# All 18 input projection blocks of a layer in 512-column products by twos, and six weight subtractions on GpSimd

## The chip, the cores and the metric

The kernel runs on one core of a Trainium2 chip. The metric is the device time of one execution, in microseconds (us). A core has a matrix engine (TensorE, in the profile PE, with its weight loads as PEld), three engines for elementwise work (VectorE or DVE, ScalarE or ACT, GpSimd or POOL), and SyncE (SP), which here issues the transfers. Each engine takes its instructions in its own order and waits at semaphores for the others. SBUF is the on-chip memory; PSUM holds the banks that TensorE writes into.

## What is computed

Two decoder layers over 256 tokens of width 1024. Each layer multiplies x by one wide input matrix and cuts the product into ten parts for three groups of heads: retention (rq, rk, rv, rg), softmax attention with a bias (mq, mk, mv) and a short convolution (cb, cc, ch). The group results go through an output matrix and a LayerNorm, then through a gated MLP and a second LayerNorm. Cut to what matters here:

```python
def hybrid_mixer(h, w_in, conv_w, w_out, rel_bias):
    proj = h @ w_in
    rq, rk, rv, rg, mq, mk, mv, cb, cc, ch = parts      # columns of proj
    q_r = rotary(split_heads(rq)); k_r = rotary(split_heads(rk)) * scale
    y_ret = merge_heads(head_group_norm(retention(q_r, k_r, v_r))) * silu(rg)
    y_moba = merge_heads(moba_attention(split_heads(mq), split_heads(mk), split_heads(mv), rel_bias))
    y_conv = cb * causal_dwconv(cc * ch, conv_w)
    return concatenate([y_ret, y_moba, y_conv]) @ w_out

def reference(x, ...):
    for l in range(2):
        x = layer_norm(ALPHA * x + hybrid_mixer(x, ...), ln1_g[l], ln1_b[l])
        x = layer_norm(ALPHA * x + conv_ffn(x, ...), ln2_g[l], ln2_b[l])
    return x
```

## The kernel before

The products keep fp32 accuracy by taking each operand as two parts in a shorter format: hi, a cast on ScalarE (`split`, line 81), and lo, what is left, a subtraction on VectorE (line 82). A product is then hi·hi + hi·lo + lo·hi. The tokens x lie in one tile `xx` of 128 rows x 8 k x 2 parts x 256 tokens; `xh` and `xl` are its two parts.

The weights come as a list of units of up to 128x1024. `prepare` (line 120) loads and converts units in the order of that list: a transfer on SP into one of five `raw` buffers, then `convert` (line 115) with `split` into one of six `whi` and six `wlo` buffers. `weights` (line 143) hands out one unit and prepares up to five units ahead.

Of each layer's input products, 18 are blocks of 128 features by 256 tokens (`FBLK`: mq0 to mq2, mk0 to mk2, then rq and rk by turns, then ch0, cc0, cb0, ch1, cc1, cb1). One block is eight steps k of the width 1024, each with three products of 256 columns into one PSUM bank `acc`, of which only the lower half is used. `feature_block` (line 311) does this for mq and mk (and a few blocks of the MLP); `block_in_halves` (line 400), a generator that stops once in the middle, does it for rq, rk (in `projections`, line 368) and ch, cc, cb (in `short_conv`, line 412), and for the first block of the MLP, up(2, 0). What uses a block reads the bank directly: line 353, 354 and 358 with the `split` behind them, `rotary` (line 390) with four ScalarE copies `sw` and two VectorE products, line 417 (`hsb`), 422 and 433.

The order of the work is fixed by the loop of lines 501 to 514: after mq and mk come `moba_scores`, `moba_transpose`, `moba_values` and `retention_scores` in turn, and between them `fill` draws pieces of the generator `bulk`, which runs through rq0, rk0, ... and the short convolution. `retention_scores(j)` reads the pair `ret[j]`, whose last part is `narrow_lo` (line 383: cast of y on ScalarE, subtraction on VectorE; in the profile `pair<-y` and `pair<-y,pair` with 128x128). Line 271 loads another activation table there. After the blocks comes rg, four units of 128x768.

In the up loop, `wide_block` (line 636) has the other form: for two steps k at a time two products hi·[xh xl] of 512 columns, then two products lo·xh of 256 columns into the upper half of the bank; a ScalarE copy and a VectorE addition bring the halves together.

Which instructions of different helpers come first on one engine is decided by a scheduler while the kernel is built, not by the source alone. PSUM has four banks `acc` and four `att`.

Of the kernel before, what the change touches and what calls it, by code (L numbers as in the profile page):

```python
# [10 lines left out]
F32 = mybir.dt.float32  # L11
# [5 lines left out]
P = 128  # L17
D = 1024
T = 256
# [7 lines left out]
KD = D // P  # L27
# [6 lines left out]

FBLK = ["mq0", "mq1", "mq2", "mk0", "mk1", "mk2", "rq0", "rk0", "rq1", "rk1", "rq2", "rk2",
        "ch0", "cc0", "cb0", "ch1", "cc1", "cb1"]
VG = ((0, 512), (512, 768))
WO_ORDER = (6, 7, 3, 4, 5, 0, 1, 2)
SLOTS = 6
# [12 lines left out]
def hybrid_decoder(ctx: ExitStack, tc: tile.TileContext, x, xw, wva, wvb, wf, wt, w_out, wg, w_up, w_down,  # L52
                   conv_w, ffn_w, ln1_g, ln1_b, ln2_g, ln2_b, rel_bias,
                   c_ident, c_rot, c_decay, out):
    nc = tc.nc
# [4 lines left out]
    sp = ctx.enter_context(tc.tile_pool(name="sp", bufs=4))  # L60
# [4 lines left out]
    def acc():  # L65
        return pa.tile([P, 512], F32, name="acc", tag="acc")

    def att():
        return pb.tile([P, 512], F32, name="att", tag="att")

    def big(dtype, name):
        return wp.tile([P, 1024], dtype, name=name, tag="big", bufs=2 * TAIL)
# [7 lines left out]
    def split(dst_hi, dst_lo, src):  # L80
        nc.scalar.copy(dst_hi, src)  # L81
        return nc.vector.tensor_sub(dst_lo, src, dst_hi.bitcast(F32))  # L82
# [30 lines left out]
    state = {"next": 0}  # L113

    def convert(key, hi, lo, r, n):
        m = n // 2 if key[1] in ("up", "dn") and key[2] < 4 else n
        for c in range(0, n, m):
            split(hi[:, c:c + m], lo[:, c:c + m], r[:, c:c + m])

    def prepare(upto):  # L120
        while state["next"] < min(upto, len(units)):
            key, src, held = units[state["next"]]
            r = raw()
            if held:
                hi, lo = big(F32R, "hhi"), big(F32R, "hlo")
            else:
                hi = wp.tile([P, 1024], F32R, name="whi", tag="whi", bufs=SLOTS)
                lo = wp.tile([P, 1024], F32R, name="wlo", tag="wlo", bufs=SLOTS)
            if state["next"] < KD:
                load_first(state["next"], r, src, hi, lo)  # L130
            elif len(src.shape) == 2:
                nc.sync.dma_start(r, src)
                convert(key, hi, lo, r, 1024)
            else:
                k, c = src.shape[1:]
                nc.sync.dma_start(r[:, :k * c].rearrange("p (k c) -> p k c", k=k), src)
                convert(key, hi, lo, r, k * c)
            ready[key] = (hi, lo)
            state["next"] += 1
            if state["next"] >= 7 and spread:  # L140
                spread.pop(0)()

    def weights(*key, ahead=LOOKAHEAD):
        prepare(index[key] + 1 + ahead)
        return ready.pop(key)


    def parts():

        x = xp.tile([P, KD, 2, T], F32R, name="xx", tag="xx")  # L150
        return x, x[:, :, 0, :], x[:, :, 1, :]

    xx, xh, xl = parts()
# [73 lines left out]
    def mirrored(src, n):  # L227

        return bass.AP(tensor=src.tensor, offset=src.offset + P - 1, ap=[list(src.ap[0]), [P, n], [-1, P]])
# [51 lines left out]
    vt = [big(F32, "v") for _ in range(NT)]  # L281
    banks = [[acc() for _ in range(NT)] for _ in VG]
    for k in range(KD):
        hi, lo = weights(0, "v", k)
        for g in (1, 0):
            n, c = VG[g][1] - VG[g][0], slice(0, T) if g else slice(T, 3 * T)
            for t in range(NT):
# [5 lines left out]
    for g in (1, 0):  # L293
        a, b = VG[g]
        for t in range(NT):
            nc.scalar.copy(vt[t][:, a:b], banks[g][t][:, :b - a])

    for l in range(DEPTH):
        def token_group(name):
# [8 lines left out]
                            k == 0, k == KD - 1)  # L308
            return ps

        def feature_block(*name):
            hi, lo = weights(l, *name)
            ps = acc()
            for k in range(KD):
                c = slice(k * P, k * P + P)
                nc.tensor.matmul(ps[:, :T], hi[:, c], xh[:, k, :], start=k == 0, stop=False)  # L316
                nc.tensor.matmul(ps[:, :T], hi[:, c], xl[:, k, :], start=False, stop=False)  # L317
                nc.tensor.matmul(ps[:, :T], lo[:, c], xh[:, k, :], start=False, stop=k == KD - 1)  # L318
            return ps
# [26 lines left out]
        def buf256(name):  # L346
            return ap.tile([P, T], F32, name=name, tag="b256", bufs=3)

        moba = [Pair() for _ in range(3)]
        for i, m in enumerate(moba):  # L350
            p = feature_block(f"mq{i}")[:, :T]
            q = buf256("q")
            nc.scalar.mul(m.narrow[:, None, :], mirrored(p[:, :P], 1), HD ** -0.5)
            nc.scalar.mul(q[:, None, :P], mirrored(p[:, P:], 1), HD ** -0.5)
            split(m.narrow_hi, m.narrow_lo, q[:, :P])
        for i, m in enumerate(moba):
            p = feature_block(f"mk{i}")[:, :T]
            nc.scalar.copy(m.wide, p[:, :P])
            split(m.wide_hi, m.wide_lo, p)
        if l == 0:  # L360
# [39 lines left out]
        def block_in_halves(key, result, ahead=LOOKAHEAD):  # L400
            hi, lo = weights(l, *key, ahead=ahead)
            ps = acc()
            for k in range(KD):
                c = slice(k * P, k * P + P)
                nc.tensor.matmul(ps[:, :T], hi[:, c], xh[:, k, :], start=k == 0, stop=False)  # L405
                nc.tensor.matmul(ps[:, :T], hi[:, c], xl[:, k, :], start=False, stop=False)  # L406
                nc.tensor.matmul(ps[:, :T], lo[:, c], xh[:, k, :], start=False, stop=k == KD - 1)  # L407
                if k == KD // 2 - 1:
                    yield
            result.append(ps[:, :T])  # L410

        def short_conv(i):
            p = []
# [119 lines left out]
        for t, p in enumerate(token_group("rg")):  # L533
            c, g = slice(t * HW, t * HW + HW), slice(t * NH, t * NH + NH)
            y, gt = yn[:, c], gate[:, c]
# [10 lines left out]
        ps = [[acc() for _ in range(2)] for _ in range(NT)]  # L546
# [9 lines left out]
        for n, k in enumerate(WO_ORDER[:-TAIL]):  # L556
            hi, lo = weights(l, "wo", k)
# [8 lines left out]
        xx, xh, xl = parts()  # L566
# [67 lines left out]
            return hh, hl  # L634

        def wide_block(*name):


            hi, lo = weights(l, *name)
            ps = acc()  # L640
            for k in range(0, KD, 2):
                for j in (k, k + 1):
                    nc.tensor.matmul(ps, hi[:, j * P:j * P + P], xx[:, j].rearrange("p s t -> p (s t)"),  # L643
                                     start=j == 0, stop=False)
                for j in (k, k + 1):
                    nc.tensor.matmul(ps[:, T:], lo[:, j * P:j * P + P], xx[:, j, 0, :],  # L646
                                     start=False, stop=j == KD - 1)
            y = buf256("feat")
            nc.scalar.copy(y, ps[:, T:])
            nc.vector.tensor_add(y, ps[:, :T], y)  # L650
            return y

        def up(f):
            if f in WIDE:
                a = wide_block("up", f, 0)
                return gated(f, a, wide_block("up", f, 1))
            a = feature_block("up", f, 0)[:, :T]
            return gated(f, a, feature_block("up", f, 1)[:, :T])
# [8 lines left out]
        ps = [[att() for _ in range(2)] for _ in range(NT)]  # L667

        def value_group(vt, vw, g, t):

            bank = []

            def step(k):
                if k == 0:
                    bank.append(acc())
                n, per = VG[g][1] - VG[g][0], KD // len(vw[g])
                hi, lo = vw[g][k // per]
                c = slice(k % per * n, k % per * n + n)
                mm3(bank[0][:, :n], xh[:, k, tokens(t)], xl[:, k, tokens(t)], hi[:, c], lo[:, c],
                    k == 0, k == KD - 1)  # L680
                if k == KD - 1:
                    nc.scalar.copy(vt[t][:, VG[g][0]:VG[g][1]], bank[0][:, :n])
            return [lambda k=k: step(k) for k in range(KD)]
# [14 lines left out]
        if l + 1 < DEPTH:  # L698
# [3 lines left out]
            xx, xh, xl = parts()  # L702
# [6 lines left out]
            for t in range(NT):  # L709
                steps = []  # L710
                for g in range(len(VG)):
                    steps += value_group(vt, vw, g, t)
# [87 lines left out]
```

## Time and profile before

| what | value |
| --- | --- |
| median of three runs | 613.96 us (613.69 to 614.12) |
| the profiled execution's own time | 614.47 us |
| its span | 612.7 us |
| TensorE busy | 603.2 us (98%) |
| VectorE busy | 458.5 us (75%) |
| ScalarE busy | 355.1 us (58%) |
| GpSimd busy | 23.2 us (4%) |
| granted TensorE clock, mean | 0.995 |

The span goes from the first to the last instruction of the profiled execution; some 1.8 us of its time lie around it. The busy shares are means over all stages of two layers, so a stage in which ScalarE is full doesn't show in them. A timeline row gives the start in the span, the busy time, the engine, the line of the kernel, the operation and its tiles, how many like instructions the row holds, and in brackets how long the engine was idle before and what ended that. Matmuls follow one another before the last has ended, so the distance of two starts, not the busy time, says what one costs.

### The profile page before, as it was taken

To read this page: it belongs to the slowest core of one execution; us is meant where nothing else is said; L and a number is where in the kernel's file an instruction comes from. 1 tells how busy PE (TensorE), PEld (TensorE's weight loads), DVE (VectorE), ACT (ScalarE), POOL (GpSimd) and SP (SyncE) were. 2 spreads that over 40 slices of the span, in tenths; PEclk is the share of its full clock that TensorE was granted. 3 is DMA by queue.
4 is the path that set the end of the run, shared out by engine and by line. 5 is a ranking of instruction groups with operands and counts; after the bars stand their busy time and mean duration, and the time that the engine had idled before them with its cause. 6 is when DMAs were issued, how large, how long until landed. Compare 5 with 4: busy or idle time off the path is not lost.

```text
span 612.7 us, 10003 instructions
## 1 busy us (share of the span) xinstructions
PE 603.2 (98%) x3748; PEld 531.7 (87%) x3748; DVE 458.5 (75%) x844; ACT 355.1 (58%) x649; POOL 23.2 (4%) x51
## 2 busy tenths in 40 slices
PE   8999999999999999999999999999999999999994
PEld 7999998888888888888889999987888888888893
DVE  5478889787667676779865788878866777777766
ACT  6579847255555656567346795552665655556620
POOL 1500010000000000000000000101000000000001
PEclk9999999999999999999999999999999999999998
DMA  8987357465655565668337425573755665665501
GB/s 301 370 286 255 96 168 244 165 214 198 199 183 193 186 188 189 199 222 296 107 102 264 149 80 170 192 250 104 239 183 196 187 190 186 193 201 176 174 1 68
DMA packets 33595, 115.87 MB, mean 189 GB/s; under 512 B 3910, under 2 KB 4684, under 8 KB 33548
## 3 DMA queue, kind: packets, MB, share of 16 engines
q1 hardware_dynamic: 33276, 114.45, 57.0%
q0 software_dynamic: 272, 0.80, 0.4%
q8 instruction: 29, 0.48, 0.3%
q14 instruction: 18, 0.15, 0.1%
HBM read 114.17 MB, written 1.06 MB: 188 GB/s over the span
## 4 chain that ended last, share of the span: by engine, by line
PE 98%; DVE 1%; DMA 0%; issue 0%; ACT 0%; DVEq 0%; SPq 0%
PE acc L643 22%; PE acc L646 11%; PE att L232 7%; PE acc L232 7%; PE att L233 7%; PE att L234 7%; PE acc L233 6%; PE acc L234 6%; PE acc L405 4%; PE acc L406 4%; PE acc L407 4%; PE acc L317 3%; PE acc L316 3%; PE acc L318 3%; PE att L344 1%; PE att L278 1%
## 5 line engine op out<-in xcount | busy, mean ns | idle before, releaser
L82 DVE TENSOR_TENSOR wlo<-raw,whi 128x1024 fp32r<-128x1024 f32 (+3 forms) x207 | 228.8, 1114 | 81.8 <-ACT whi L81 80.5
L81 ACT CAST whi<-raw 128x1024 fp32r<-128x1024 f32 (+3 forms) x207 | 197.2, 963 | 93.9 <-PE acc L643 39.4
L643 PE MATMUL acc<-xx,whi 128*128 128x512 f32 x576 | 180.9, 395 | 0.0
L646 PEld LDWEIGHTS acc<-xx,wlo 128*128 128x128 f32 x576 | 108.2, 188 | 25.2
L646 PE MATMUL acc<-xx,wlo 128*128 128x256 f32 x576 | 113.5, 278 | 0.0
L643 PEld LDWEIGHTS acc<-xx,whi 128*128 128x128 f32 x576 | 90.3, 189 | 2.7
L405 PE MATMUL acc<-xx,whi 128*128 128x256 f32 x208 | 60.1, 289 | 0.0
L406 PE MATMUL acc<-xx,whi 128*128 128x256 f32 x208 | 58.8, 283 | 0.0
L407 PE MATMUL acc<-xx,wlo 128*128 128x256 f32 x208 | 58.8, 283 | 0.0
L233 PE MATMUL att<-whi,hl 128*128 128x512 f32 x144 | 56.3, 391 | 0.0
L234 PE MATMUL att<-wlo,hh 128*128 128x512 f32 x144 | 56.0, 389 | 0.0
L232 PE MATMUL att<-whi,hh 128*128 128x512 f32 x144 | 55.5, 392 | 0.0
L232 PE MATMUL acc<-whi,xx 128*128 128x512 f32 (+2 forms) x128 | 46.6, 366 | 0.5 <-ACT whi L81 0.5
L233 PE MATMUL acc<-whi,xx 128*128 128x512 f32 (+2 forms) x128 | 45.8, 359 | 0.0
L234 PE MATMUL acc<-wlo,xx 128*128 128x512 f32 (+2 forms) x128 | 45.1, 357 | 0.0
L623 ACT ACTIVATE za<-feat,fw 128x256 f32<-128x256 f32 x36 | 18.4, 510 | 40.8 <-DVE feat L650 40.7
L317 PE MATMUL acc<-xx,whi 128*128 128x256 f32 x144 | 40.8, 283 | 0.0
L318 PE MATMUL acc<-xx,wlo 128*128 128x256 f32 x144 | 40.8, 283 | 0.0
L316 PE MATMUL acc<-xx,whi 128*128 128x256 f32 x144 | 40.7, 283 | 0.0
L405 PEld LDWEIGHTS acc<-xx,whi 128*128 128x128 f32 x208 | 39.8, 191 | 0.7
L406 PEld LDWEIGHTS acc<-xx,whi 128*128 128x128 f32 x208 | 39.9, 192 | 0.1
L407 PEld LDWEIGHTS acc<-xx,wlo 128*128 128x128 f32 x208 | 39.8, 191 | 0.0
(137 smaller groups left out, 938.5 us busy)
## 6 DMA issues: line engine op xcount, KB each, us to landing
raw<-in_w_up_dram SPq DMA_DIRECT2D x80, 512.0 KB, 4.4
raw<-in_w_down_dram SPq DMA_DIRECT2D x44, 512.0 KB, 4.4
raw<-in_wf_dram SPq DMA_DIRECT2D x36, 512.0 KB, 4.7
raw<-in_w_out_dram SPq DMA_DIRECT2D x16, 512.0 KB, 3.8
raw<-in_wg_dram SPq DMA_DIRECT2D x8, 512.0 KB, 4.4
raw<-in_xw_dram SPq DMA_DIRECT2D x7, 512.0 KB, 5.8
raw<-in_wt_dram SPq DMA_DIRECT2D x8, 384.0 KB, 3.3
lnp<-in_ln_g_dram SPq DMA_DIRECT2D x4, 512.0 KB, 3.4
```

Source lines behind the costliest of these rows:

```text
L81: nc.scalar.copy(dst_hi, src)
L82: return nc.vector.tensor_sub(dst_lo, src, dst_hi.bitcast(F32))
L232: nc.tensor.matmul(ps, lhi, rhi, start=first, stop=False)
L233: nc.tensor.matmul(ps, llo, rhi, start=False, stop=False)
L234: nc.tensor.matmul(ps, lhi, rlo, start=False, stop=last)
L317: nc.tensor.matmul(ps[:, :T], hi[:, c], xl[:, k, :], start=False, stop=False)
L318: nc.tensor.matmul(ps[:, :T], lo[:, c], xh[:, k, :], start=False, stop=k == KD - 1)
L405: nc.tensor.matmul(ps[:, :T], hi[:, c], xh[:, k, :], start=k == 0, stop=False)
L406: nc.tensor.matmul(ps[:, :T], hi[:, c], xl[:, k, :], start=False, stop=False)
L407: nc.tensor.matmul(ps[:, :T], lo[:, c], xh[:, k, :], start=False, stop=k == KD - 1)
L643: nc.tensor.matmul(ps, hi[:, j * P:j * P + P], xx[:, j].rearrange("p s t -> p (s t)"), start=j == 0, stop=False)
L646: nc.tensor.matmul(ps[:, T:], lo[:, j * P:j * P + P], xx[:, j, 0, :], start=False, stop=j == KD - 1)
```

## The change

All 18 input blocks of each layer, and up(2, 0), take the pairwise form of the up loop. A new function `both` issues it, and `wide_block` uses it too. A new function `halves` copies the upper half of the bank into a tile `small` on ScalarE and adds it onto the lower half, in the bank, on VectorE; the users read the bank after that. `input_block` takes the place of `feature_block` for mq and mk, and `block_in_halves` ends with `halves`. The units of `BY_POOL`, six of each layer (mk2, rk0, rk1, rk2, cc0, ch1), are still cast on ScalarE, but the subtraction goes to GpSimd.

```diff
+BY_POOL = FBLK[5:16:2]
...
     def convert(key, hi, lo, r, n):
+        if key[1] in BY_POOL:
+            nc.scalar.copy(hi, r)
+            nc.gpsimd.tensor_sub(lo, r, hi.bitcast(F32))
+            return
...
+        def both(ps, hi, lo, tiles):
+            for k in tiles:
+                nc.tensor.matmul(ps, hi[:, k * P:k * P + P], xx[:, k].rearrange("p s t -> p (s t)"),
+                                 start=k == 0, stop=False)
+            for k in tiles:
+                nc.tensor.matmul(ps[:, T:], lo[:, k * P:k * P + P], xx[:, k, 0, :], start=False, stop=k == KD - 1)
+
+        def halves(ps):
+            y = sp.tile([P, T], F32, name="small", tag="f256", bufs=6)
+            nc.scalar.copy(y, ps[:, T:])
+            nc.vector.tensor_add(ps[:, :T], ps[:, :T], y)
+            return ps[:, :T]
+
+        def input_block(*name):
+            hi, lo = weights(l, *name)
+            ps = acc()
+            for k in range(0, KD, 2):
+                both(ps, hi, lo, (k, k + 1))
+            return halves(ps)
...
-            p = feature_block(f"mq{i}")[:, :T]
+            p = input_block(f"mq{i}")
...
-            p = feature_block(f"mk{i}")[:, :T]
+            p = input_block(f"mk{i}")
...
         def block_in_halves(key, result, ahead=LOOKAHEAD):
...
-            for k in range(KD):
-                c = slice(k * P, k * P + P)
-                nc.tensor.matmul(ps[:, :T], hi[:, c], xh[:, k, :], start=k == 0, stop=False)
-                nc.tensor.matmul(ps[:, :T], hi[:, c], xl[:, k, :], start=False, stop=False)
-                nc.tensor.matmul(ps[:, :T], lo[:, c], xh[:, k, :], start=False, stop=k == KD - 1)
-                if k == KD // 2 - 1:
+            for k in range(0, KD, 2):
+                both(ps, hi, lo, (k, k + 1))
+                if k == KD // 2 - 2:
                     yield
-            result.append(ps[:, :T])
+            result.append(halves(ps))
```

The order of instructions changes on the elementwise engines too. The rows below name line, operation, tiles with the number of their buffer, and shape. The place is the end of the first layer's third retention pair: `y` with 128x128 is what `rotary` made of rk2, `pair` from it is the last part that `retention_scores(2)` needs, `whi` and `wlo` with 128x768 are units of rg, `hsb` and `small` belong to ch0. On ScalarE, before:

```order
L271 ACTIVATE table_992<-prob_852 128x1
L81 CAST pair_576<-y_954 128x128
L417 COPY hsb_1025<-acc_1000 128x256
L81 CAST whi_1028<-raw_1027 128x768
L81 CAST whi_1104<-raw_1103 128x768
```

and after:

```order
L276 ACTIVATE table_932<-prob_802 128x1
L328 COPY small_957<-acc_940 128x256
L82 CAST whi_963<-raw_962 128x768
L82 CAST pair_546<-y_894 128x128
L82 CAST whi_1034<-raw_1033 128x768
L442 COPY hsb_960<-acc_940 128x256
```

The cast of the pair stood right behind the activation table; now ch0's small copy and one cast of a unit of rg stand between. On VectorE at the same place, before:

```order
L396 TENSOR_TENSOR sw_946<-sw_946,rot_82 128x256
L397 TENSOR_TENSOR a_947<-acc_921,rot_82 128x256
L381 TENSOR_TENSOR y_954<-a_947,sw_946 128x128
L382 TENSOR_TENSOR plain_577<-a_947,sw_946 128x128
L82 TENSOR_TENSOR pair_576<-y_954,pair_576 128x128
L82 TENSOR_TENSOR wlo_1029<-raw_1027,whi_1028 128x768
```

and after:

```order
L424 TENSOR_TENSOR sw_886<-sw_886,rot_82 128x256
L425 TENSOR_TENSOR a_887<-acc_866,rot_82 128x256
L409 TENSOR_TENSOR y_894<-a_887,sw_886 128x128
L410 TENSOR_TENSOR plain_547<-a_887,sw_886 128x128
L329 TENSOR_TENSOR acc_940<-acc_940,small_957 128x256
L83 TENSOR_TENSOR wlo_964<-raw_962,whi_963 128x768
L83 TENSOR_TENSOR pair_546<-y_894,pair_546 128x128
```

The subtraction of the unit of rg has moved from behind the pair's subtraction to ahead of it, and ch0's addition stands there too.

## Rows read from the trace of the kernel before

**Rows 1.** The page: busy us (share) and instructions; the chain by engine.

```profile
PE 603.2 (98%) x3748; PEld 531.7 (87%) x3748; DVE 458.5 (75%) x844; ACT 355.1 (58%) x649; POOL 23.2 (4%) x51
...
PE 98%; DVE 1%; DMA 0%; issue 0%; ACT 0%; DVEq 0%; SPq 0%
```

**Rows 2.** Windows: us; busy (x) of PE, PEld, DVE, ACT, POOL; clock; DMA; GB/s.

```profile
58.00:75.00 17.00, 17.00 (x157) 15.83 (x156) 14.24 (x43) 16.14 (x40) 0.00 (x0) 1.00 0.39 112
...
604.00:612.00 8.00, 0.78 (x4) 0.31 (x2) 4.52 (x9) 0.00 (x0) 0.92 (x1) 0.67 0.20 70
```

**Rows 3.** Timeline of ScalarE, first layer, 33 to 74 us.

```profile
33.11 1.04 ACT L81 CAST whi<-raw 128x1024 fp32r<-128x1024 f32 x1
...
41.06 0.27 ACT L358 COPY plain<-acc 128x128 f32<-128x128 f32 x1 [0.44 <-PE acc L318]
...
68.95 0.30 ACT L378 COPY plain<-y 128x128 f32<-128x128 f32 x1 [0.47 <-DVE y L377]
...
72.50 0.28 ACT L81 CAST pair<-y 128x128 fp32r<-128x128 f32 x1
72.81 0.37 ACT L417 COPY hsb<-acc 128x256 f32<-128x256 f32 x1
73.07 1.57 ACT L81 CAST whi<-raw 128x768 fp32r<-128x768 f32 x2
```

**Rows 4.** Timeline of VectorE, first layer, the last retention pair's low part.

```profile
72.81 0.29 DVE L82 TENSOR_TENSOR pair<-y,pair 128x128 fp32r<-128x128 f32 x1 [0.42 <-ACT pair L81]
73.94 0.96 DVE L82 TENSOR_TENSOR wlo<-raw,whi 128x768 fp32r<-128x768 f32 x1 [0.84 <-ACT whi L81]
```

**Rows 5.** Timeline of TensorE, first layer, the last retention pair's scores.

```profile
73.12 0.60 PE L344 MATMUL att<-pair 64*128 64x256 f32 x6
73.65 0.39 PE L405 MATMUL acc<-xx,whi 128*128 128x256 f32 x1
```

**Rows 6.** Timeline of ScalarE, second layer, 341 to 373 us.

```profile
341.00 1.05 ACT L81 CAST whi<-raw 128x1024 fp32r<-128x1024 f32 x1 [1.39 <-PE acc L317]
...
343.88 0.40 ACT L456 ACTIVATE prob<-prob,sm 128x128 f32<-128x128 f32 x1 [1.40 <-DVE sm L454]
...
371.62 0.28 ACT L81 CAST pair<-y 128x128 fp32r<-128x128 f32 x1
371.80 0.83 ACT L81 CAST whi<-raw 128x768 fp32r<-128x768 f32 x1
372.54 0.36 ACT L417 COPY hsb<-acc 128x256 f32<-128x256 f32 x1
```

**Rows 7.** Timelines of VectorE and TensorE, second layer, the same place.

```profile
371.93 0.29 DVE L82 TENSOR_TENSOR pair<-y,pair 128x128 fp32r<-128x128 f32 x1 [0.31 <-ACT pair L81]
...
372.94 0.60 PE L344 MATMUL att<-pair 64*128 64x256 f32 x6
373.47 0.39 PE L405 MATMUL acc<-xx,whi 128*128 128x256 f32 x1
```

**Rows 8.** Timeline of TensorE, first layer, mk2: the first products of two k.

```profile
37.99 0.28 PE L316 MATMUL acc<-xx,whi 128*128 128x256 f32 x1
...
38.35 0.28 PE L316 MATMUL acc<-xx,whi 128*128 128x256 f32 x1
```

**Rows 9.** Timeline of TensorE, up loop: the second product of a pair onward.

```profile
146.46 0.63 PE L643 MATMUL acc<-xx,whi 128*128 128x512 f32 x2
...
149.25 0.63 PE L643 MATMUL acc<-xx,whi 128*128 128x512 f32 x2
```

**Rows 10.** Groups by line and shape, VectorE: busy us, mean ns; idle before.

```profile
L82 DVE TENSOR_TENSOR wlo<-raw,whi 128x1024 fp32r<-128x1024 f32 x158 | 192.5, 1223 | 73.1 <-ACT whi L81 72.2
...
L650 DVE TENSOR_TENSOR feat<-acc,feat 128x256 f32<-128x256 f32 x72 | 30.0, 417 | 0.8 <-ACT feat L649 0.8
```

**Rows 11.** Groups by line and shape, GpSimd: busy us, mean ns; idle before.

```profile
L192 POOL COPY row<-rel 6x143 f32<-6x143 f32 x1 | 0.3, 293 | 0.0
...
L192 POOL COPY row<-rel 6x14 f32<-6x14 f32 x1 | 0.2, 186 | 0.0
```

More of the change, by code (lines that the diff above doesn't have):

```diff
@@ L641, in wide_block @@
             for k in range(0, KD, 2):
[L642 to L647, printed above, removed]
+                both(ps, hi, lo, (k, k + 1))
             y = buf256("feat")
```

## The prediction

> **What bounds the kernel now.** I read the page first: TensorE is busy 98% of the span, and 98% of the chain that ended last is TensorE [rows 1]. So the time is the sum of the matmuls, and anything that shortens them pays, as long as nobody else becomes late. Then the windows, to see whom TensorE could find late. In the stretch 58 to 75 us (the second half of the first layer's attention part) ScalarE is busy 16.14 of 17.00 us [rows 2]. Third, ScalarE's timeline. In the first layer it waits 0.44 us at 41.06 us, and after that for nothing but the 0.47 us at 68.95 us, up to the cast of the last retention pair at 72.50 us [rows 3]. An engine that always has the next operation waiting is behind: whatever is added to its queue in there moves its end. TensorE reaches the scores of that pair at 73.12 us, and the pair's low part is finished 0.29 us after 72.81 us, at 73.10 us [rows 4, 5]. So the first layer has no slack at this place. In the second layer ScalarE waits 1.40 us at 343.88 us and is full from there; the low part starts at 371.93 us, ends at 372.22, and TensorE comes at 372.94: some 0.7 us of slack [rows 6, 7]. The reader is to see that a program bound by TensorE has one place in each layer at which a queue of ScalarE ends just in time.
>
> **What shorter products give.** A block before takes three 256-column products for each of eight k. The first products of two k stand 38.35 - 37.99 = 0.36 us apart, so 2.88 us a block [rows 8]. The pairwise form runs already in the up loop: four pairs from 146.46 to 149.25 us, 2.79 us a block [rows 9]. Each block saves 0.09 us; 19 blocks a layer (18 input blocks and the first up block) and two layers are 38, so 38 x 0.09 = 3.4 us, if TensorE never waits. The gain is this small since the number of columns is unchanged: 2 x 512 + 2 x 256 against 6 x 256; only gaps between products go.
>
> **What it costs.** The product now lies in two halves of a bank. Each block needs a copy of 128x256 on ScalarE (0.26 us from one start to the next: 72.81 to 73.07 [rows 3]) and an addition on VectorE (0.417 us in the like row of the up loop [rows 10]) before anyone can use the result. VectorE gets six subtractions of 1.22 us a layer off [rows 10] and has room. ScalarE gets nothing off, since the casts of the six weights stay on it. This is where I expect the loss.
>
> First layer, start of the last pair's cast: 72.50 us before. The six blocks ahead of the full stretch end 6 x 0.09 = 0.54 us earlier, and so it begins earlier. Between there and the pair's cast, eight small copies are added (mk2, three rq, three rk, ch0): 8 x 0.26 = 2.08 us. The order of ScalarE also puts one cast of a 768-column rg weight ahead of the pair's cast, where before it stood behind: 0.74 us (371.80 to 372.54 in the second layer [rows 6]). The 0.47 us of waiting can be filled. So 72.50 - 0.54 + 2.08 + 0.74 - 0.47 = 74.3 us; 74.8 if the wait stays. On VectorE the order turns too: the 768-column subtraction (0.96 us; it began 0.87 us after its cast had begun [rows 3, 4]) now stands ahead of the pair's. The 768 cast begins 0.74 us before the pair's cast, at 73.6 to 74.1; its subtraction begins 0.87 later, at 74.4 to 74.9, and ends near 75.4 to 75.9; the pair's low part then ends 0.29 later, 75.7 to 76.2. Two thirds of six products of 0.53 us in all still need it (0.35 us): the scores end at 76.0 to 76.5 us, against 73.65 [rows 5]. I take 2.3 us of delay, near the lower end, as a queue that is late fills small gaps that no row shows. Behind that only four input blocks and the first up block are shorter: 5 x 0.09 = 0.45. The first layer: +2.3 - 0.45 = +1.9 us. What the other blocks saved is eaten by the wait.
>
> Second layer: from the cast at 341.00 to the pair's cast at 371.62 are 30.62 us [rows 6]. It begins 0.54 earlier (340.46), takes eight copies (2.08), the 768 cast (0.74) and now also the copy of hsb (0.26) ahead, and fills perhaps 0.9 of the 1.40 us of waiting: 340.46 + 30.62 + 2.08 + 0.74 + 0.26 - 0.9 = 373.3 us. Before, the pair's subtraction began 0.31 us after its cast had begun [rows 6, 7]; the 768 subtraction of VectorE is ahead again and ends about then or a little later, so the low part ends near 374.2 and the scores near 374.6, against 373.47: +1.1 - 0.45 = +0.65 us. Bounds: 0 (the slack holds) to +1.2.
>
> Sum: +1.9 + 0.65 = +2.5 us, on the profiled execution's own 614.47 about 617.0; that run is 0.5 us above the median of 613.96, so **616.4 us**.
>
> **GpSimd's subtractions.** No row of before shows GpSimd subtract 1024 elements. The nearest: copies of 143 and 14 elements take 293 and 186 ns [rows 11], 0.83 ns an element, so about 1.0 us for 1024 with one input; the upper bound, two such inputs, 2.0 us. A gain against VectorE's 1.22 is excluded by nothing, but it would change no end. I take the upper one, since a subtraction reads two. Cover: mk2's weight cast starts at 33.11 us, takes 1.04 [rows 3], and its first low product begins near 38.2, so 4.1 us for the subtraction; 2.0 fit. Later weights stand up to five blocks ahead. Uncovered it would cost a wait of TensorE of what exceeds that cover.
>
> The Trainium skill, "GPSIMD Engine Reference", section 3.1, gives 4497 ns on GpSimd against 2293 on VectorE for a 2048-element fp32 tensor_tensor, and advises VectorE for elementwise work; halved, that is an estimate of 2.25 us, and it speaks against this change. By it the cover of 4.1 us still holds, and the sum would stay where it is.
>
> **Rivals.** (1) *The queue has more room than it shows* (no change). ScalarE's records are full, but small waits between operations may hide in them, and the delay of 2.3 us may be 1, the second layer's 0: +1.0 - 0.45 - 0.45 = +0.1, with the late-run remainder some 614.6 us. For it: hidden gaps of 0.02 to 0.1 us between dozens of operations. Against: 2.8 us are added to a queue that waited 0.47.
> (2) *Faster: TensorE stays dense.* If ScalarE's added 2.8 us are absorbed before 72.5 us, all 3.4 us remain: 613.96 - 3.4 = 610.5 us. Place: the pair's low part in both layers; it decides if ScalarE has at least 2.5 us of room in the first layer's full stretch. Against it, the window's 16.14 of 17.00 us busy.
> (3) *GpSimd and VectorE keep each other waiting.* If every GpSimd subtraction holds VectorE up for its whole 2.0 us, the two that fall next to a late chain (rk0's and ch1's) add about 1.0 us each in that stretch, where VectorE is busy 14.24 of 17.00 [rows 2]: 616.4 + 2.0 = 618.4 us. Nothing in the trace speaks for or against, as GpSimd does nothing in that stretch [rows 2].
> The Trainium skill, "SBUF — State Buffer", section "Who interferes with whom", says that a VectorE operation with two SBUF inputs and a GpSimd operation that reads SBUF exclude each other for a whole instruction; no row of before shows it.
> (4) *The clock falls.* In 604 to 612 us, where TensorE idles, the granted clock is 0.67 [rows 2]. A wait of 2 us, followed by some us at half clock, would make it 619 to 620. Waits this short inside dense work stand in no row of before.
>
> **How the numbers follow.** The forecast, 616.4, gets 0.52; its own range is 615.2 to 617.4 (the lower and upper ends above: +1.2 to +3.5). Rival 1, 614.6, 0.18; rival 2, 610.5, 0.12; rival 3, 618.4, 0.14; rival 4, 0.04. The range 613.2 to 618.8 leaves out rival 2, rival 4 and a little of the third. A measurement of this kernel can tell about 0.2%, 1.2 us, from no change: same means 612.7 to 615.2. Faster 0.12; same 0.22 (rival 1 and the forecast's low end); slower 0.66.
>
> **What the profile after would show.** Right: blocks of 2.79 us; ScalarE's pair cast of the last retention pair past 74 us in the first layer and past 373 in the second; TensorE waiting 1 to 3 us ahead of the low products of that pair's scores, released by VectorE's pair; dense work elsewhere. GpSimd's share rises by twelve subtractions of some 2 us. Wrong: no wait of TensorE at those scores (rival 2), or waits ahead of other blocks, for GpSimd's wlo or for VectorE's sums; VectorE's subtractions longer than 1.22 us beside GpSimd's (rival 3); a granted clock under 1.0 behind the wait (rival 4). If pair casts come at 73 us, ScalarE had the room that I deny it.

## The result, and the profile after

The changed kernel takes 623.01 us (median of five runs, 621.01 to 624.11), the kernel before 614.08 us; the ratio is 1.0138 (95% interval 1.0125 to 1.0151). It is 8.9 us slower, where 2.5 us had been forecast; the time lies above the range.

The page of the changed kernel, busy time and the chain that ended last, to be read against [rows 1]:

```profile
PE 607.1 (98%) x3444; PEld 518.3 (83%) x3444; DVE 471.3 (76%) x870; ACT 362.7 (58%) x687; POOL 52.9 (9%) x63
...
PE 84%; ACT 9%; DVE 4%; issue 2%; DMA 0%; DVEq 0%; SPq 0%; ACTq 0%
```

The share of busy time of TensorE is unchanged, but its share of the chain has gone from 98% to 84%: for 9% of the span the chain now runs through ScalarE, for 4% through VectorE. Where, the starts of TensorE's rows tell. I cut each layer into two stages: **A** from the first input block to the first scores of the softmax attention (the six mq and mk blocks), **B** from there to the start of the retention values (`att<-v,rs`; ten of the other twelve blocks lie in it). In the first layer B runs from 40.95 to 79.59 us before and from 40.91 to 84.63 after. A and B are from the one profiled execution of each kernel, in us.

| kernel | A, layers 1 and 2 | B, layer 1 | B, layer 2 | median of runs, beside before |
| --- | --- | --- | --- | --- |
| before | 17.36, 17.37 | 38.64 | 38.39 | 614.08 |
| changed | 16.80, 16.82 | 43.72 | 43.78 | 623.01 |

A is 0.56 us shorter in each layer, as six blocks of 2.79 instead of 2.88 us should be. B is 5.1 and 5.4 us longer. Nothing else of the program has changed by as much as 1 us. So all of the loss lies in the two stretches in which ScalarE is full. In the first layer TensorE's timeline names the places (line 493 is the transposes of the softmax, 372 the scores, 320 the blocks):

```profile
41.15 0.60 PE L372 MATMUL att<-pair 64*128 64x256 f32 x6
41.68 0.73 PE L320 MATMUL acc<-xx,whi 128*128 128x512 f32 x2
...
48.23 0.88 PE L493 MATMUL att<-ident,prob 128*128 128x128 f32 x6
48.86 0.71 PE L320 MATMUL acc<-xx,whi 128*128 128x512 f32 x2
...
51.04 0.63 PE L320 MATMUL acc<-xx,whi 128*128 128x512 f32 x2
...
55.66 0.60 PE L372 MATMUL att<-pair 64*128 64x256 f32 x6
56.91 1.56 PE L493 MATMUL att<-ident,prob 128*128 128x128 f32 x6 [0.64 <-DVE prob L486]
58.23 0.71 PE L320 MATMUL acc<-xx,whi 128*128 128x512 f32 x2
...
65.17 0.60 PE L372 MATMUL att<-pair 64*128 64x256 f32 x6
67.09 1.80 PE L493 MATMUL att<-ident,prob 128*128 128x128 f32 x6 [1.32 <-DVE prob L486]
68.55 1.20 PE L320 MATMUL acc<-xx,whi 128*128 128x512 f32 x2
69.97 1.05 PE L320 MATMUL acc<-xx,whi 128*128 128x512 f32 x2
71.25 0.82 PE L320 MATMUL acc<-xx,whi 128*128 128x512 f32 x2
72.15 0.63 PE L320 MATMUL acc<-xx,whi 128*128 128x512 f32 x2
...
77.42 0.38 PE L372 MATMUL att<-pair 64*128 64x256 f32 x2
78.42 0.50 PE L372 MATMUL att<-pair 64*128 64x256 f32 x4 [0.61 <-DVE pair L83]
78.86 0.73 PE L320 MATMUL acc<-xx,whi 128*128 128x512 f32 x2
```

Undisturbed, the six products of scores take 0.53 us and the six transposes 0.63 (41.15 to 41.68 and 48.23 to 48.86, the first rows). So the second transposes should have let the next block start at 55.66 + 1.16 = 56.82; it starts at 58.23, 1.4 us late. At the third it is 68.55 instead of 66.33, 2.2 us late. Behind them three pairs of steps take 72.15 - 68.55 = 3.60 us, where 2.18 is usual (48.86 to 51.04): 1.4 us, and the reason is in the windows below. The last pair's scores, the one place that the prediction named, come 1.0 us late on their own: from the scores before them to the next block it is 2.09 us (76.77 to 78.86), where it was 1.10 before (72.55 to 73.65). Sum 6.0 us, against 5.1 longer and 0.9 saved by ten shorter blocks. The second layer gives, by the same reckoning, 0.3 and 1.3 us at the transposes, 0.9 ahead of two halves of blocks, 2.0 at the last scores and 1.5 behind them. Ahead of one of these halves (374.76 us) TensorE waits 0.59 us for the rotary product `a`, which reads a block's bank: by this row it waits for a bank to come free.

Windows of the changed kernel, two us each (columns as in [rows 2]):

```profile
66.00:68.00 2.00, 0.78 (x4) 0.39 (x4) 1.89 (x10) 1.51 (x5) 0.00 (x0) 1.00 0.58 181
68.00:70.00 2.00, 2.00 (x8) 1.68 (x9) 1.85 (x4) 1.95 (x5) 0.00 (x0) 0.56 0.00 0
70.00:72.00 2.00, 2.00 (x8) 1.67 (x8) 1.78 (x6) 1.96 (x6) 0.00 (x0) 0.58 0.55 108
...
380.00:382.00 2.00, 1.17 (x11) 0.87 (x12) 2.00 (x6) 1.80 (x5) 0.00 (x0) 1.00 0.00 0
382.00:384.00 2.00, 2.00 (x7) 1.66 (x8) 2.00 (x6) 0.00 (x0) 0.00 (x0) 0.57 0.87 279
384.00:386.00 2.00, 2.00 (x9) 1.76 (x8) 2.00 (x8) 0.00 (x0) 0.00 (x0) 0.58 0.77 240
```

Behind the longest wait of each layer the granted clock is 0.56 to 0.58 for four us: most of that time at the lower level, 1.2 GHz. TensorE is busy all through, but does little more than half of its work. Before the change, the clock falls only at the end of the program.

What holds the transposes up is seen where GpSimd and VectorE are read side by side. First GpSimd's timeline, then VectorE's, first layer:

```profile
47.73 2.44 POOL L119 TENSOR_TENSOR wlo<-raw,whi 128x1024 fp32r<-128x1024 f32 x1 [2.35 <-ACT whi L118]
52.58 2.40 POOL L119 TENSOR_TENSOR wlo<-raw,whi 128x1024 fp32r<-128x1024 f32 x1 [2.40 <-ACT whi L118]
62.42 2.40 POOL L119 TENSOR_TENSOR wlo<-raw,whi 128x1024 fp32r<-128x1024 f32 x1 [7.44 <-ACT whi L118]
```

```profile
48.90 2.35 DVE L83 TENSOR_TENSOR wlo<-raw,whi 128x1024 fp32r<-128x1024 f32 x1 [0.51 <-ACT whi L82]
...
53.27 0.41 DVE L479 CUSTOM_DVE_ANT_0 prob<-att,bias 128x256 f32<-128x256 f32 x1
...
53.62 1.64 DVE L83 TENSOR_TENSOR pair<-y,pair 128x256 fp32r<-128x256 f32 x1
...
62.87 2.22 DVE L83 TENSOR_TENSOR pair<-y,pair 128x256 fp32r<-128x256 f32 x1 [0.42 <-ACT pair L82]
65.02 0.41 DVE L479 CUSTOM_DVE_ANT_0 prob<-att,bias 128x256 f32<-128x256 f32 x1
```

GpSimd's three end at 50.17, 54.98 and 64.82 us; VectorE's three end at 51.25, 55.26 and 65.09: 1.1, 0.3 and 0.3 us after GpSimd, somewhat under the 1.2 and 0.4 us that such an operation is busy when alone. They begin on the record when their inputs are there, but run only when GpSimd has ended. The operation at 53.27, which reads one input from PSUM, takes its usual 0.41 us in the middle of GpSimd's. The last row is the damage: the softmax's minimum, an operation that runs beside GpSimd at 53.27, stands in VectorE's queue behind the pair's subtraction and starts 2.2 us after it, where 0.34 is usual (51.58 to 51.92 before); the last exponential on ScalarE, the scaling (line 486) and the transposes at 67.09 are late with it.

### The profile page after: what moved, and what is told of

Read it like the earlier page. It is cut to its first block, busy times and chain, and to the rows that moved or that the text cites. A ratio compares the mean times of both kernels' runs of the same rounds, so it can differ in the third digit from the quotient of the medians.

```text
span 621.8 us, 9490 instructions
## 1 busy us (share of the span) xinstructions
PE 607.1 (98%) x3444; PEld 518.3 (83%) x3444; DVE 471.3 (76%) x870; ACT 362.7 (58%) x687; POOL 52.9 (9%) x63
## 4 chain that ended last, share of the span: by engine, by line
PE 84%; ACT 9%; DVE 4%; issue 2%; DMA 0%; DVEq 0%; SPq 0%; ACTq 0%
PE acc L320 27%; PE acc L323 13%; PE att L237 7%; PE acc L237 7%; PE att L238 6%; PE att L239 6%; PE acc L238 6%; PE acc L239 6%; ACT whi L82 2%; ACT sw L423 2%; ACT prob L481 1%; DVE wlo L83 1%; PE att L283 1%; DVE pair L83 1%; ACT whi L118 1%
## 5 line engine op out<-in xcount | busy, mean ns | idle before, releaser
L320 PE MATMUL acc<-xx,whi 128*128 128x512 f32 x880 | 280.0, 399 | 0.6 <-DVE a L425 0.6
L323 PEld LDWEIGHTS acc<-xx,wlo 128*128 128x128 f32 x880 | 166.6, 189 | 39.2
L323 PE MATMUL acc<-xx,wlo 128*128 128x256 f32 x880 | 174.5, 279 | 0.0
L320 PEld LDWEIGHTS acc<-xx,whi 128*128 128x128 f32 x880 | 138.2, 191 | 4.7 <-ACT cath L82 0.8
L119 POOL TENSOR_TENSOR wlo<-raw,whi 128x1024 fp32r<-128x1024 f32 x12 | 29.4, 2451 | 58.4 <-ACT whi L118 58.4
L239 PEld LDWEIGHTS att<-wlo,hh 128*128 128x128 f32 x144 | 27.0, 188 | 5.7
L238 PEld LDWEIGHTS att<-whi,hl 128*128 128x128 f32 x144 | 27.0, 188 | 4.7 <-DVE hl L83 0.3
L237 PEld LDWEIGHTS att<-whi,hh 128*128 128x128 f32 x144 | 26.9, 188 | 4.9 <-ACT hh L82 0.5
L668 DVE TENSOR_TENSOR feat<-acc,feat 128x256 f32<-128x256 f32 x72 | 30.1, 418 | 0.8 <-ACT feat L667 0.8
L83 DVE TENSOR_TENSOR hl<-hf,hh 128x256 fp32r<-128x256 f32 x44 | 18.6, 423 | 14.1 <-ACT hh L82 13.7
L237 PEld LDWEIGHTS acc<-whi,xx 128*128 128x128 f32 x128 | 24.9, 195 | 4.3 <-ACT whi L82 1.3
```

The costliest lines, as they stand in the source:

```text
L119: nc.gpsimd.tensor_sub(lo, r, hi.bitcast(F32))
L237: nc.tensor.matmul(ps, lhi, rhi, start=first, stop=False)
L238: nc.tensor.matmul(ps, llo, rhi, start=False, stop=False)
L239: nc.tensor.matmul(ps, lhi, rlo, start=False, stop=last)
L320: nc.tensor.matmul(ps, hi[:, k * P:k * P + P], xx[:, k].rearrange("p s t -> p (s t)"), start=k == 0, stop=False)
L323: nc.tensor.matmul(ps[:, T:], lo[:, k * P:k * P + P], xx[:, k, 0, :], start=False, stop=k == KD - 1)
```

## The experiments

Each label stands for one kernel; times are medians, beside the median of before at that point (614.0 to 614.4). B is from the profiled execution alone, whose own time was up to 1.5 us off the median (e1 620.92, e4 621.18, f1 616.16), so the B columns add up to the last one only roughly.

| run | B, layer 1 | B, layer 2 | median | against before |
| --- | --- | --- | --- | --- |
| e1: changed, all subtractions on VectorE | 41.64 | 42.53 | 619.54 | +5.5 |
| e2: before, six subtractions on GpSimd | 42.08 | 38.72 | 618.10 | +4.1 |
| h1: the same in four pieces each | 39.70 | 38.40 | 614.81 | +0.6 |
| i1: changed, GpSimd in four pieces | 43.00 | 43.02 | 621.33 | +6.9 |
| e3: pairwise in mq, mk alone | 40.63 | 39.07 | 615.85 | +1.8 |
| e4: pairwise in the other blocks alone | 41.57 | 42.06 | 619.66 | +5.6 |
| c1: before, extra ScalarE copies | 39.98 | 40.14 | 617.04 | +2.6 |
| f1: e1, rg held behind the last pair | 41.06 | 39.71 | 617.06 | +2.6 |
| f3: changed, rg held behind | 42.64 | 41.65 | 619.67 | +5.3 |
| f2: e3, rg held behind | 40.01 | 39.06 | 615.52 | +1.1 |
| g1: pairwise in five blocks, rg and hsb held | 38.73 | 38.92 | 614.27 | +0.1 |
| g2: pairwise in three blocks, rg and hsb held | 39.26 | 38.40 | 614.14 | 0.0 |

**Undoing and isolating GpSimd's part.** Two theories went in. L: GpSimd and VectorE hold each other up. Q: ScalarE's longer queue is the loss, as in the prediction. e1 empties `BY_POOL` in the changed kernel; e2 puts the change's GpSimd branch of `convert` into the kernel before and changes nothing else.

```diff
-BY_POOL = FBLK[5:16:2]
+BY_POOL = []
```

> The changed kernel with all weight subtractions back on VectorE (BY_POOL empty); products, copies and additions as changed. Theory L (GpSimd's subtractions of 2.4 us and VectorE's two-input operations hold each other up, and the last scores of each pair wait for that): VectorE's 256-column pair subtractions are back at 0.43 us, and the time falls by 4 us or more, to 616 to 619. Theory Q (the eight small copies and the early rg cast in ScalarE's queue are the loss, GpSimd is not): VectorE gets 7 us a layer more to do and nothing is gained, 621 to 624. Under both the last pair's cast stays late, since here the order puts two 768-column casts ahead of it.

> The kernel before, with the one part that six weight subtractions a layer go to GpSimd; all products in 256 columns, no small copies. Theory L: VectorE's operations with two SBUF inputs wait up to 1.8 us beside GpSimd's, with little more queued than before: slower by 1 to 4 us, 615 to 618, and single pair subtractions of 1 to 2 us in the trace. Theory Q: ScalarE's queue is as before and VectorE is 7 us a layer lighter: 613.5 to 614.5, same.

e1 took 619.54 us, 0.5 above L's range and 1.5 below Q's; e2 took 618.10, just above L's range and 3.6 above Q's. The subtractions on GpSimd alone, which take work off VectorE and put none on ScalarE, cost 4.1 us, 3.4 of it in B of the first layer. Theory Q's "same" for e2 has fallen. But e1 also shows that without GpSimd 5.5 us of loss remain. So both are at work. How much of the 3.5 us between the changed kernel and e1 is GpSimd's can't be read from this pair, since the order on ScalarE and VectorE differs too; the next pairs keep it.

**One GpSimd instruction or four.** What in GpSimd's part costs: that a weight is ready later, or that VectorE stands still for one whole instruction?

```diff
-            nc.gpsimd.tensor_sub(lo, r, hi.bitcast(F32))
+            for c in range(0, n, 256):
+                nc.gpsimd.tensor_sub(lo[:, c:c + 256], r[:, c:c + 256], hi[:, c:c + 256].bitcast(F32))
```

> The kernel before with six subtractions a layer on GpSimd, as in the run that took 618.1, but each in four pieces of 256 columns. Theory L (VectorE's operation waits until the one GpSimd instruction ends): a wait is at most some 0.65 us instead of up to 2, so VectorE's 256-column pair subtractions fall from up to 2.4 us to at most 1.1, and the time to 615 to 616.5. If GpSimd's slowness itself is the price (a weight that is ready 1.2 us later), the total per weight grows a little and the time stays at 618 or more.

614.81 us, a little under theory L's range: of 4.1 us, 0.6 are left. The pair's subtraction on VectorE, grouped by line and shape (busy us, mean ns, idle before), in the kernel before, in e2 and in h1; last what GpSimd took in h1:

```profile
L82 DVE TENSOR_TENSOR pair<-y,pair 128x256 fp32r<-128x256 f32 x6 | 2.5, 422 | 0.4 <-ACT pair L81 0.3
```

```profile
L83 DVE TENSOR_TENSOR pair<-y,pair 128x256 fp32r<-128x256 f32 x6 | 10.2, 1704 | 0.3 <-ACT pair L82 0.2
```

```profile
L83 DVE TENSOR_TENSOR pair<-y,pair 128x256 fp32r<-128x256 f32 x6 | 3.6, 594 | 0.3 <-ACT pair L82 0.2
```

```profile
L120 POOL TENSOR_TENSOR wlo<-raw,whi 128x256 fp32r<-128x256 f32 x48 | 39.2, 849 | 44.5 <-ACT whi L118 44.5
```

The mean goes from 422 to 1704 ns and back to 594, while GpSimd as a whole takes longer in pieces (39.2 us against 30.7). In both layers' stretch B up to the last scores ScalarE and VectorE run the same operations in the same order in e2 and h1. So GpSimd's slowness is not the price; the length of a single instruction is.

The same edit in the changed kernel:

> The changed kernel with one change: each of the twelve GpSimd subtractions in four pieces of 256 columns. Theory L and Q together: the part of the loss that comes with GpSimd's whole instructions, 3.3 us (the difference of the four-piece run and the whole-piece run without pairwise products), goes, and the queue's and the order's part stays: 619 to 620.5 against 623.0. If with pairwise products VectorE's waits beside GpSimd are hidden behind ScalarE's late queue anyway, 622 to 623.

621.33 us, 1.7 less than 623.01, not 3.3: between the two expectations. The 1.7 isn't clear of the changed kernel's own spread, as two of its five runs took 621.01 and 621.36. In i1's trace the pair's subtraction is back at 486 ns, so most of VectorE's waits there are gone, and the order of operations is that of the changed kernel; but TensorE still waits at the transposes and the last scores of both layers. In this trace the clock falls once (378 to 384 us), not twice. Losses that lie beside each other need not add.

**A longer queue, without sums and without GpSimd.** One more ScalarE copy behind each bulk block of the kernel before, with nobody reading the result:

```diff
+            y = sp.tile([P, T], F32, name="small", tag="f256", bufs=6)
+            nc.scalar.copy(y, ps[:, :T])
             result.append(ps[:, :T])
```

> The kernel before, with one more 128x256 ScalarE copy behind each of the 13 blocks of rq to cb and up(2, 0), whose result nobody reads; order at the end of the attention part as before, the last pair ahead of the rg weights. Measures the queue's length alone. Theory Q: seven copies stand ahead of the last pair's cast, 7 x 0.26 = 1.8 us less 0.47 of waiting: first layer +1.3 us, second layer 0 to 0.5 (slack 0.7 and 1.4 us of waiting), 615.2 to 616.0. Theory O (not the queue's length, but the new dependence copy, addition, user and the new order at the end): 613.7 to 614.5, same.

617.04 us, 1.0 above theory Q's range and 2.5 above theory O's (O: what costs is the new chain of copy, addition and user, and the new order at the end). B grows by 1.34 us in the first layer, the 1.3 expected, and by 1.75 in the second, where 0 to 0.5 was. The last pair's cast in the first layer starts at 73.27 us, with a start of the first block 0.63 earlier than in the kernel before: 73.9 on its clock, where 72.50 + 1.82 - 0.47 = 73.85 follows. In the second layer the wait is elsewhere, at the transposes of the softmax (TensorE's timeline of c1):

```profile
365.29 0.60 PE L344 MATMUL att<-pair 64*128 64x256 f32 x6
367.09 1.36 PE L470 MATMUL att<-ident,prob 128*128 128x128 f32 x6 [1.20 <-DVE prob L463]
```

But there the copies are not all that changed. ScalarE's timeline, first of the kernel before, then of c1, at the exponentials of this softmax:

```profile
361.25 0.40 ACT L456 ACTIVATE prob<-prob,sm 128x128 f32<-128x128 f32 x1
362.00 0.51 ACT L456 ACTIVATE prob<-prob,sm 128x256 f32<-128x256 f32 x1
```

```profile
363.95 0.40 ACT L458 ACTIVATE prob<-prob,sm 128x128 f32<-128x128 f32 x1
364.35 1.03 ACT L81 CAST whi<-raw 128x1024 fp32r<-128x1024 f32 x1
365.28 0.51 ACT L458 ACTIVATE prob<-prob,sm 128x256 f32<-128x256 f32 x1
```

Before, only the cast of a pair lies between the two; in c1 a weight's cast stands there, 0.93 us from its start to the next, and on VectorE its subtraction (365.41 us) ahead of the scaling. The same cast has moved in the first layer (61.88 us). So c1 shows that more copies make the kernel late without GpSimd, and where, but it doesn't part the queue's length from the order that the scheduler makes of it.

**The order at the end of the stretch.** f1 and f3 hold the casts and subtractions of the rg weights behind the last pair's cast and subtraction (`issue_after` keeps the order on one engine; it adds no wait):

```diff
-                        split(m.narrow_hi, m.narrow_lo, y[:, :P])
+                        state["hi"] = nc.scalar.copy(m.narrow_hi, y[:, :P])
+                        state["lo"] = nc.vector.tensor_sub(m.narrow_lo, y[:, :P], m.narrow_hi.bitcast(F32))
...
+        if key[1] == "rg":
+            with behind(state["hi"]):
+                nc.scalar.copy(hi[:, :n], r[:, :n])
+            with behind(state["lo"]):
+                nc.vector.tensor_sub(lo[:, :n], r[:, :n], hi[:, :n].bitcast(F32))
+            return
```

> All blocks pairwise, all subtractions on VectorE, and the rg weights' casts and subtractions held behind the last pair's cast and subtraction on their engines; the kernel without that hold took 619.5. Theory O: two casts of 0.74 and a subtraction of 0.88 us go from ahead of the last pair: 1.5 us less a layer, 616 to 617. Theory Q: the queue is as long as before up to the transposes and scores ahead of it, where the waits arise; the end follows, and at most 1 us in all comes back, 618.5 to 619.5.

> The changed kernel (with GpSimd's subtractions) with the same hold of the rg weights: one cast of 0.74 and one subtraction of 0.88 us go from ahead of the last pair in each layer. Theory O: 1 to 1.6 us less a layer, 620 to 621. If the low part waits for something else that is late by then, 622.5 to 623.5.

f1 took 617.06 us, 2.5 less than e1, at the upper end of what theory O said; f3 619.67, 3.3 less than the changed kernel, more than expected. In both pairs one fall of the granted clock is gone from the traces as well (e1 has one, at 378 to 384 us, f1 none in B; the changed kernel two, f3 one). By the cost read in the changed kernel a fall is worth some 1.5 us, an estimate. The order at the end is a real cost, and part of it seems to be paid through the clock.

**Which blocks.** Pairwise products in the six mq and mk blocks alone, in the others alone, and then versions meant to win: mq and mk with rg held; five blocks without mk2; three blocks. No GpSimd in any.

> Pairwise products in the six mq and mk blocks of each layer only, everything else and all subtractions as before. ScalarE waits over 1 us a block there, so the copies are covered. Both theories: 12 blocks x 0.09 us = 1.1 us faster than before, 612.9, with no wait of TensorE in the first six blocks. If the shorter start is eaten by ScalarE's full queue behind it (the last retention pair's low part comes no earlier), 613.9, same.

> Pairwise products in the twelve rq to cb blocks and up(2, 0) only, mq and mk as before, all subtractions on VectorE. Theory Q: the copies in ScalarE's full stretch are the loss; the time is that of the kernel with all blocks pairwise and VectorE's subtractions, or up to 1.1 us above it, 616 to 620. Theory L without GpSimd: TensorE's 26 blocks x 0.09 = 2.3 us are gained as far as no wait eats them: 612 to 615.

> Pairwise products in the six mq and mk blocks alone and the rg weights held behind the last pair; without the hold it took 615.85. Theory O: the 0.74 us cast and the 0.88 us subtraction leave the path of the first layer, and with 1.1 us of shorter products the time is 613 to 614. Theory Q: the copies' 0.26 us are what counts, 615 to 616.

> Pairwise products in mq0 to mq2, mk0 and mk1 only (mk2 in the old form, so that no small copy stands behind the start of ScalarE's full stretch), all subtractions on VectorE, the rg weights and the hsb copy held behind the last pair's cast. No added work in the full stretch: if the queue's length and order are all that counts, 10 blocks x 0.09 = 0.9 us are gained, 613.0 to 613.6 against 614.0 to 614.4 of before. If the stretch still lengthens (first layer by more than 0.9 us), the scheduler's other moves cost as much, 614 to 615.5.

> The same with pairwise products in mq0 to mq2 only. Queue and order theory: 6 blocks x 0.09 = 0.5 us, 613.5 to 613.9. Against the run with five blocks it tells whether what is lost comes with mk0's and mk1's copies.

e3 missed: 615.85, 1.8 us slower than before, where both theories said 1.1 faster. A was 0.56 us shorter in both layers, as expected, but B 2.0 us longer in the first: mk2's copy and addition stand at the head of the full stretch, and the order at its end has turned here too. ScalarE's timeline of e3 shows an rg cast and the copy of `hsb` ahead of the last pair's cast, which [rows 3] has behind:

```profile
71.61 0.37 ACT L445 COPY hsb<-acc 128x256 f32<-128x256 f32 x1
71.88 0.84 ACT L82 CAST whi<-raw 128x768 fp32r<-128x768 f32 x1
72.74 0.30 ACT L82 CAST pair<-y 128x128 fp32r<-128x128 f32 x1
```

With the hold (f2) it took 615.52, where theory Q had it and not O (613 to 614): here the order at the end was worth little. With mk2 in the old form and `hsb` held too (g1) it took 614.27, with mq alone (g2) 614.14: no gain can be measured, where 0.9 and 0.5 us were expected. The ratio to before is 1.0004 (0.9995 to 1.0013) for g1 and 1.0001 (0.9992 to 1.0010) for g2. What A gains, 0.3 to 0.5 us a layer, B loses in one of the two layers (the second in g1, the first in g2). e4 took 619.66, inside theory Q's range and as much as e1: the six short blocks of mq and mk bring nothing there. No run beat the kernel before.

## Why the prediction was wrong, point by point

- **The shorter products: right.** 0.09 us a block, 0.56 a layer in A. No wait of TensorE was seen in A.
- **ScalarE's queue as a cause: right, and in the first layer its size too, as far as GpSimd is not in it.** c1 gave +1.34 us in the first layer where the reckoning with copies alone gives 1.3, though its order had moved a little too. In the changed kernel the last pair's cast starts at 77.07 us, 76.5 on the clock of the kernel before (its first block starts 0.52 later), against 74.3 to 74.8 predicted. ScalarE's timeline shows why:

```profile
43.48 0.27 ACT L386 COPY plain<-acc 128x128 f32<-128x128 f32 x1 [1.15 <-DVE acc L329]
...
66.47 0.30 ACT L82 CAST pair<-y 128x128 fp32r<-128x128 f32 x1 [0.71 <-DVE y L409]
...
76.07 0.37 ACT L328 COPY small<-acc 128x256 f32<-128x256 f32 x1
76.34 0.84 ACT L82 CAST whi<-raw 128x768 fp32r<-128x768 f32 x1
77.07 0.30 ACT L82 CAST pair<-y 128x128 fp32r<-128x128 f32 x1
```

- **The step that failed first: "The 0.47 us of waiting can be filled."** I took ScalarE to be waiting for nothing more. It now waits 1.15 us for VectorE's new addition and 0.71 for `y`, and both VectorE operations stand behind one that GpSimd holds up. Together that is 1.9 us, 1.4 more than the 0.44 us that it waited at the first of these places before: the larger part of the 2.2 us by which the cast is later than the 74.3 that counts the waiting as filled.
- **Second: one place instead of three.** The sum followed the queue to the last pair's scores alone. The transposes of the softmax were late by 1.4 and 2.2 us in the first layer and 0.3 and 1.3 in the second, and without GpSimd they are late too (1.3 us of waits in the first layer in e1 and in f1). The trace of the kernel before had such a place already: its first transposes take 0.87 us to the next block instead of 0.63.

```profile
48.44 1.11 PE L468 MATMUL att<-ident,prob 128*128 128x128 f32 x6
49.31 0.37 PE L405 MATMUL acc<-xx,whi 128*128 128x256 f32 x1
```

- **Third: rival 3, mutual waiting, was priced at 2.0 us with a chance of 0.14; it is real.** Alone it costs 4.1 us, of which 3.5 go when the instruction is cut in four; in the changed kernel cutting it gave 1.7, which is within the spread. That the rest is hidden there behind the late queue is argued, not shown. I had seen neither how long a whole instruction is nor that operations which need nothing of GpSimd queue behind the one that waits. Here the trace agrees with the Trainium skill, "SBUF — State Buffer", section "Who interferes with whom": a VectorE operation with two SBUF inputs and a GpSimd operation that reads SBUF exclude each other for a whole instruction; 0.4 us become 1.6 and 2.2, and one with a PSUM input stays at 0.41. The prediction cited this page and still gave the rival the smaller chance.
- **Fourth: rival 4, the clock, came on top, not instead.** It was priced as a case of its own. It came behind the longest wait of each layer, at 1.4 and 1.5 us. A wait of a dense engine can have a second price.
- **GpSimd's time: outside the bounds.** 2451 ns each, against 1.0 to 2.0 from copies. The cover held all the same: mk2's subtraction ends at 36.65 us, ahead of its first low product at 38.49, and no wait of TensorE names a weight that GpSimd made.
- **The order at the end: right as a cause,** some 1.5 us in the sum of the first layer; holding it back gave 2.5 and 3.3 us over both layers, clock included.

What stays open: f1, without GpSimd and with the rg weights held, is still 2.6 us slower than before, though its products are 3.4 us shorter, so 6.0 us are lost there. c1's bare copies, with the order that came with them, cost 2.6. If f1's copies cost as much, another 3.4 us are left to the additions on VectorE, the longer way from block to user and the rest of the order; no run took these apart. One part of the longer way is seen in f1's TensorE timeline, a wait for the copy `hsb`, which reads the bank of ch0 after the new copy and addition (in e1 it is 1.15 us):

```profile
74.04 0.74 PE L326 MATMUL acc<-xx,whi 128*128 128x512 f32 x2 [0.55 <-ACT hsb L449]
```

A block's bank is held longer in the new form, and TensorE waits for it.

## What to carry to other kernels

Before moving elementwise work to another engine, look at what runs beside it: here a GpSimd instruction of 2.4 us with SBUF inputs stopped VectorE's two-input operations and everything queued behind them, so cut such an instruction into pieces or keep it away from the critical stretch. Where an engine beside the bottleneck has been full for 30 us, an added operation can be late at every later hand-over, not at the last one alone; follow all of them, and look at what the scheduler moved. Saving 0.09 us a block on TensorE doesn't pay for 0.26 us of ScalarE and 0.42 of VectorE in a stretch where these two end just in time.

## What the runs showed of the hardware

- GpSimd took 2.40 us for a subtraction of 128x1024 in fp32 where VectorE takes 1.22; cut in four, 849 ns a piece with the waits among them.
- The holding up is mutual: a GpSimd subtraction that met a running one of VectorE took 2.97 us instead of 2.40 (first layer, 42.41 us).
- Not only operations with two tiles from SBUF are held up. Two scalings of the softmax (line 486, one tile and one column in), 0.55 us for both when alone, took 1.27 us at 349.45 us in the changed kernel, beside a GpSimd subtraction that ran from 347.97 to 350.38. Cutting doesn't free these: the mean of the 128x128 ones is 284 ns before, 344 in e2 and 368 in h1.
- After 2 us windows with TensorE busy 0.78 and 1.17 us, the granted clock stood at 0.56 to 0.58 for 4 us. In e2 a window of 2 us with 0.25 us busy was followed by full clock, so the length of a wait alone doesn't tell it; why is open. Windows of e2:

```profile
54.00:56.00 2.00, 0.25 (x3) 0.04 (x1) 2.00 (x12) 1.51 (x6) 0.00 (x0) 1.00 0.63 157
56.00:58.00 2.00, 1.54 (x10) 0.77 (x10) 1.50 (x8) 1.95 (x7) 0.00 (x0) 1.00 0.94 384
```

- The clock goes with the spread of the changed kernel's times: runs of 621.0 and 621.4 us had a mean clock of 0.997, those of 623.0 to 624.1 us 0.991.
